# Moving V's stationary tiles by 352 bytes, dealing the second tokens' top-k between the gates of the first, and plain fp32 tiles of U beside top-k and the list only

## The chip, the cores and the metric

The kernel runs on one core of a Trainium2 chip. The metric is device time in microseconds (us) of the whole program, as the median of several executions. All engine names are those of the profile: PE is TensorE's matmul, PEld its weight loads, DVE is VectorE, ACT is ScalarE, POOL is GpSimd, SP is SyncE (here only a DMA queue).

## What is computed

Two transformer blocks on 256 tokens of width 2048, all in fp32. The change lies in one part of the first block, a mixture of 16,384 experts from which each token takes 128:

```python
q = (xn @ w_pq).reshape(B, S, 8, 2, 128)
s1, s2 = q[..., 0, :] @ sub_k1.T, q[..., 1, :] @ sub_k2.T      # 128 scores each, per head
v1, i1 = top_k(s1, 16);  v2, i2 = top_k(s2, 16)
cand = v1[..., :, None] + v2[..., None, :]                      # 256 per head
vs, ci = top_k(cand, 16)
eidx = i1[ci // 16] * 128 + i2[ci % 16];  gates = softmax(vs)
act = gelu(expert_u[eidx] . x)                                  # per token and chosen expert
y   = sum(act * gates * expert_v[eidx])
```

## The kernel before

**Three stages.** The program is a list of weight steps, each with a `prep` (load, split the fp32 weights into a high part `wh` on ACT and a low part `wl` on DVE) and an `mm` (the matmuls). A `Stream` issues `prep` of the next step and then `mm` of this one. Beside it runs a `Background`: after each step `strm.adv(n, bg, budget)` lets generators issue work until the costs that they `yield` use up the budget (a debt is carried over). So the order on every engine is fixed when the program is written, and each engine takes its instructions in that order. The stages that matter here:

- **U** (128 steps, one for each 128 experts): all experts' U rows against all 256 tokens. A step loads a tile of 1 MB by SP, transposes it on DVE (L804, `uT`, two buffers), and multiplies 16 blocks of 128 x 128 with the tokens. A *split* block takes three fp32r matmuls (L830 to L832: `wh` with `xh`, `wh` with `xl`, `wl` with `xh`). A *plain* block takes one fp32 matmul of `uT` with `xf` (L825), which the trace records as two passes. A plain step has 8 plain and 8 split blocks, so its `wh` and `wl` are one tile of 1024 columns; a split step has 16 split blocks and two such tiles. Steps 0 to 63 are plain (`NFU = 64`), 64 to 127 split. After the matmuls ACT and DVE make the first half of gelu from the accumulator (L835, L836), one step later the second half (L845, L846).
- **Beside U, in the background** (`peer_gen`): top-k of tokens 0 to 127 (`pairs_gen`, `topk_gen`; DVE only, save a few rows); then for each 64 tokens the gates (`gate_gen`: per 4 tokens one-hot tiles on DVE, L1045, and ACT, L1044, and their products on PE, L1053 and L1056) and the stores of them to DRAM (`store_gen`); top-k of tokens 128 to 255 stands beside the stores; then the list of chosen experts (`lists_gen`: a chain of small steps on DVE and PE, then 16 rounds of one-hots, L1136, and 8 products, L1170); then `p_gen`, one tile.
- **V** (109 steps and one more): rows of V for the listed experts are gathered by POOL, split, and used as the moving operand, 512 columns at a time, with the gated activations `ph` and `pl` (128 x 128) as stationary operand (L892 to L894: 1956 matmuls in this run). One step for both halves of the tokens has 24 matmuls, one for one half has 12.

Two budgets and costs set how much background work a step gets: 1.3 for the 8 first steps of U, 2.2 for the next 64, 2.0 for the other 56 until the list is done; a side of 128 scores costs 1.05, a head's 256 candidates 2.1, a block of gates 1.2.

**Places in SBUF.** Tiles lie one after another in a partition, in the order in which they are first asked for. Of the tiles that TensorE reads (bytes from the partition's start, as the built program lists them):

| tile | start | remainder by 64 |
|---|---|---|
| `wh`, `wl` (4 each) | 61216 + 4096 n, 77600 + 4096 n | 32 |
| `xh`, `xl` | 93984, 110368 | 32 |
| `ph`, `pl` (5 slots, tag `t1`) | 140736 + 1024 n | 0 |
| `pph`, `ppl` (tag `g2`, the projection of p) | 145856 + 2048 n | 0 |
| `xf`, `uT` | 202752; 210944 and 219136 | 0 |

The functions that the change touches, with the profile's line numbers:

Of the kernel before, what the change touches and what calls it, by code (L numbers as in the profile page):

```python
# [12 lines left out]
F32 = mybir.dt.float32  # L13
# [12 lines left out]
NE = 128  # L26
WB = 4
NF = 8
NFU = 64
WA, WB0, WB1 = 81, 28, 110  # L30


# [57 lines left out]
def tile_kernel(ctx: ExitStack, tc: tile.TileContext, A, out, dbg=None):  # L90
    nc = tc.nc
    V, S, T, G, SP = nc.vector, nc.scalar, nc.tensor, nc.gpsimd, nc.sync
# [18 lines left out]
    def bank(tag):  # L111
        return psp.tile([128, 512], F32, tag=tag, name=tag)
# [5 lines left out]
    def split(hi, lo, src):  # L118
        S.activation(hi, src, AF.Copy)  # L119
        V.tensor_tensor(lo, src, hi.bitcast(F32), op=OP.subtract)  # L120
# [81 lines left out]
    strm = Stream()  # L202
    bg = Background()

    class GStep:
        def __init__(self, g, k):
            self.g, self.k = g, k
            self.la = 3
            self.nw = 2 if g.ncols > 1024 else 1
# [93 lines left out]
    def flat(t):  # L303
        return t.rearrange("p a b -> p (a b)")
# [439 lines left out]
    tk = p2.enter_context(tc.tile_pool(name="tk", bufs=1))  # L744
# [8 lines left out]
    def t1(dt, name):  # L753
        return tk.tile([128, 256], dt, tag="t1", name=name, bufs=5)

    def g2(shape, dt=F32, name="g2"):
        return tk.tile(shape, dt, tag="g2", name=name, bufs=5)
# [16 lines left out]
    listI = tk.tile([128, 128], U32, name="listI")  # L774
    flag = tk.tile([1, 4], F32, name="flag")
    flagI = tk.tile([1, 1], I32, name="flagI")
    ubank = [bank("acc") for _ in range(3)]
    cnt = bank("acc")
    PP = {}
# [3 lines left out]
    class UStep:  # L783
        def __init__(self, f):
            self.f = f
            self.nf = NF if f < NFU else 0
            self.nw = 1 if self.nf == 8 else 2
            self.la = 1
            self.uT = None
            steps[f] = self  # L790

        def load(self):
            e = self.f * 128
            raw = raw_tile().rearrange("p (g c) -> p g c", g=4)
            src = A["expert_u"][0, e:e + 128, :].rearrange("(g j) (s q c) -> s q j g c", g=4, s=2, q=4)
            for i in range(8):
                s, q = i // 4, i % 4
                SP.dma_start(raw[32 * q:32 * q + 32, :, 256 * s:256 * s + 256], src[s, q])
            self.raw = raw
# [41 lines left out]
    def u_finish():  # L841
        if not pend:
            return
        f, x, a = pend.pop()
        S.activation(a, a, AF.Tanh, scale=GC3)  # L845
        V.scalar_tensor_tensor(a, a, 1.0, x, op0=OP.add, op1=OP.mult)  # L846
        G.dma_start(AG[f * 128:f * 128 + 128, 0:256], a)  # L847

    class VStep:
        la = 1  # L850
        nw = 2
# [79 lines left out]
    def p_gen():  # L931
        pin = g2([128, 2, 256], name="pin")
        S.dma_start(pin, A["p"][0, 0].rearrange("(b p) c -> p b c", p=128))
        PP["h"] = g2([128, 2, 256], F32R, "pph")
        PP["l"] = g2([128, 2, 256], F32R, "ppl")
        yield 3.0
        pt = bank("ms")
        for kk in range(2):
            for tb in range(2):
                T.transpose(pt[:, kk * 256 + tb * 128:kk * 256 + (tb + 1) * 128],  # L940
                            pin[:, tb, kk * 128:(kk + 1) * 128], ident)
        split(flat(PP["h"]), flat(PP["l"]), pt)
        yield
# [26 lines left out]
    def pairs_gen(tb, grp):  # L970
        for h2 in range(2):
            s = pq2[grp][:, tb, h2 * 512:h2 * 512 + 512].rearrange("p (a b) -> p a b", a=4)
            yield from topk_pair(tb, 4 * grp + 2 * h2, s)

    def top16(vals, idx, src, n):
        tmp = g2([128, 256], name="mr")[:, :n]
        V.max(vals[:, 0:8], src)
        V.max_index(idx[:, 0:8], vals[:, 0:8], src)
        V.match_replace(tmp, vals[:, 0:8], src, NEG)
        V.max(vals[:, 8:16], tmp)  # L980
        V.max_index(idx[:, 8:16], vals[:, 8:16], tmp)

    def topk_pair(tb, h0, s):
        vsel, i12, csel = vsel2[tb], i122[tb], csel2[tb]
        for i in range(2):
            hd = h0 + i
            v12 = tk.tile([128, 2, 16], F32, tag="v12", name="v12", bufs=2)
            ix = tk.tile([128, 2, 16], U32, tag="ix", name="ix", bufs=2)
            for side in range(2):
                top16(v12[:, side], ix[:, side], s[:, 2 * i + side, :], 128)  # L990
                V.tensor_copy(i12[side][:, hd, :], ix[:, side])
                yield 1.05
            cand = g2([128, 16, 16], name="cand")
            V.tensor_tensor(cand, v12[:, 0][:, :, None].to_broadcast([128, 16, 16]),
                            v12[:, 1][:, None, :].to_broadcast([128, 16, 16]), op=OP.add)
            top16(vsel[:, hd], csel[:, hd], cand.rearrange("p a b -> p (a b)"), 256)
            yield 2.1

    def topk_gen(tb):
        vsel, i12, csel = vsel2[tb], i122[tb], csel2[tb]  # L1000
# [37 lines left out]
    def gate_gen(t0, cost):  # L1038
        def one_hots(b):
            o1 = tk.tile([128, 4, 128], F32, tag="o1", name="o1", bufs=3)  # L1040
            o2 = tk.tile([128, 4, 128], F32, tag="o2", name="o2", bufs=3)
            for j in range(4):
                t = 4 * b + j
                S.activation(o2[:, j], iotaf, AF.Square, bias=eT[:, 1, t:t + 1])  # L1044
                V.tensor_scalar(o1[:, j], iotaf, eT[:, 0, t:t + 1], gT[:, t:t + 1], op0=OP.is_equal, op1=OP.mult)  # L1045
            S.activation(flat(o2), flat(o2), AF.Relu, scale=-1.0, bias=1.0)
            return o1, o2

        def products(b, oh):
            acc = bank("ms")  # L1050
            o1, o2 = oh
            for j in range(4):
                T.matmul(acc[:, j * 128:(j + 1) * 128], o2[:, j], o1[:, j], start=True, stop=True)  # L1053
            for j in range(4):
                t = (4 * b + j) % 128
                T.matmul(cnt[:, 128 * tb:128 * tb + 128], o2[:, j].bitcast(BF16)[:, 1::2], o1[:, j].bitcast(BF16)[:, 1::2],  # L1056
                         start=(t == 0), stop=(t == 127))
            return acc

        def place(b, acc):  # L1060
            S.activation(GB[:, :, 4 * b:4 * b + 4], acc.rearrange("p (t f) -> p f t", t=4), AF.Copy)

        tb, b0 = t0 // 128, t0 // 4
        ohs = []
        for i in range(2):
            ohs.append(one_hots(b0 + i))
            yield cost
        for b in range(16):
            acc = products(b0 + b, ohs.pop(0))
            if b < 14:  # L1070
                ohs.append(one_hots(b0 + b + 2))
            yield cost
            place(b, acc)

    def store_gen(t0, cost):
        dst = AG.rearrange("(f e) c -> e f c", e=128)
        for i in range(16):
            G.dma_start(dst[:, 8 * i:8 * i + 8, 256 + t0:320 + t0], GB[:, 8 * i:8 * i + 8, :])
            yield cost
# [104 lines left out]
    def both_gen(a, b, na, nb):  # L1184
        a, b = iter(a), iter(b)
        live = True
        while live:
            live = False
            for it, n in ((a, na), (b, nb)):
                for _ in range(n):  # L1190
                    c = next(it, None)
                    if c is not None:
                        live = True
                        yield c

    def chain(*gens):
        for g in gens:
            yield from g

    def peer_gen():  # L1200
        yield from chain(pairs_gen(0, 0), scores_gen(1), pairs_gen(0, 1), topk_gen(0))
        rest = chain(pairs_gen(1, 0), pairs_gen(1, 1), topk_gen(1))
        yield from gate_gen(0, 1.2)
        yield from both_gen(store_gen(0, 0.1), islice(rest, 14), 1, 1)
        yield from gate_gen(64, 1.2)
        yield from both_gen(store_gen(64, 0.1), rest, 1, 2)
        yield from gate_gen(128, 1.2)
        yield from store_gen(128, 0.6)
        yield from gate_gen(192, 1.2)
        yield from both_gen(store_gen(192, 0.2), lists_gen(), 1, 1)  # L1210
        yield from p_gen()

    def xs_gen():
# [28 lines left out]
    for k in range(8):  # L1242
        xs.one()
        strm.adv(1, bg, 0.7)
    bg.drain()
    bg.add(peer_gen())
    strm.adv(8, bg, 1.3)
    strm.adv(NFU, bg, 2.2)
    strm.adv(NE - NFU, bg, 2.0)
    u_finish()  # L1250
    bg.drain()

# [266 lines left out]
    for i in range(2):  # L1519
# [4 lines left out]
    rest = (tk.tile([128, 512], F32, tag="o1", name="ag", bufs=3),  # L1524
            big.tile([128, 2048], F32, tag="uT", name="rest", bufs=2), t1(F32R, "ph"), t1(F32R, "pl"))
# [116 lines left out]
```

## Time and profile before

| | |
|---|---|
| median of 3 runs | 2581.96 us (2581.3 to 2583.01) |
| the profiled execution | 2583.29 us, of which 2581.6 us is the span from first to last instruction |
| mean granted TensorE clock | 0.993 |
| PE busy | 2508.2 us, 97% |
| PEld busy | 2182.6 us, 85% |
| DVE busy | 1850.1 us, 72% |
| ACT busy | 1330.5 us, 52% |
| POOL busy | 398.4 us, 15% |

Matmuls are pipelined: the next one starts before the last one's recorded end, so PE counts as busy though it may start matmuls at different rates. Times within a stage are therefore read below as the distance from one start to the next. U's matmuls run from 391.9 to 1311.7 us, V's from 1326.0 to 1792.1 us.

### The profile page before, as it was taken

The numbers are of one execution on the slowest core, as the hardware profiler recorded it, in microseconds if no ns is written. First come the engines' busy times: TensorE is split into PE (matmuls) and PEld (weight loads), VectorE is DVE, ScalarE is ACT, GpSimd is POOL, SyncE is SP. The second block draws the span as 40 slices with busy tenths as digits, with TensorE's granted clock in tenths as the row PEclk, the third lists the DMA queues.
The fourth block names the chain that finished last, engine by engine and source line by source line (L and its number), as shares of the span: only waits on it lengthen the run. The fifth ranks groups of instructions, "written<-read, shape, count | busy, mean of one in ns | idle before, by whom it ended". The sixth has DMA issues, their size and how long they took to land. (4 is left out here: it accounts for less than half of the span.)

```text
span 2581.6 us, 37994 instructions
## 1 busy us (share of the span) xinstructions
PE 2508.2 (97%) x14001; PEld 2182.6 (85%) x14001; DVE 1850.1 (72%) x2851; ACT 1330.5 (52%) x2183; POOL 398.4 (15%) x529
## 2 busy tenths in 40 slices
PE   9999999999999999999899999999999999999999
PEld 8877778899898899898878888887888888888887
DVE  5665678987969989899957777776666456754564
ACT  6765543255362486645445555555555555544443
POOL 3000000001201202011035555552000000000000
PEclk9999999999999999999999999999999999999999
DMA  6644786665756768577679988997555545555664
GB/s 222 188 136 148 184 174 159 165 175 157 224 140 195 223 162 244 149 199 201 165 254 316 319 313 318 317 320 249 179 191 193 179 163 185 191 180 189 185 191 153
DMA packets 247154, 528.91 MB, mean 205 GB/s; under 512 B 27704, under 2 KB 163856, under 8 KB 232624
## 3 DMA queue, kind: packets, MB, share of 16 engines
q1 hardware_dynamic: 206864, 344.54, 45.3%
q0 software_dynamic: 36528, 179.96, 20.2%
q10 hardware_dynamic: 3568, 1.91, 0.3%
q8 instruction: 111, 1.82, 0.3%
q14 instruction: 83, 0.68, 0.1%
HBM read 488.55 MB, written 37.75 MB: 204 GB/s over the span
## 5 line engine op out<-in xcount | busy, mean ns | idle before, releaser
L120 DVE TENSOR_TENSOR wl<-raw,wh 128x1024 fp32r<-128x1024 f32 (+4 forms) x640 | 737.3, 1170 | 379.4 <-ACT wh L119 353.9
L119 ACT ACTIVATE wh<-raw 128x1024 fp32r<-128x1024 f32 (+4 forms) x640 | 637.2, 1010 | 380.5 <-PE acc L247 279.2
L832 PE MATMUL acc<-xh,wl 128*128 128x256 f32 x1536 | 438.8, 286 | 30.6 <-DVE wl L819 30.1
L245 PE MATMUL acc<-wh,xh 128*128 128x512 f32 (+2 forms) x1152 | 456.6, 396 | 6.0 <-ACT h L406 4.2
L830 PE MATMUL acc<-xh,wh 128*128 128x256 f32 x1536 | 451.3, 294 | 0.0
L246 PE MATMUL acc<-wl,xh 128*128 128x512 f32 (+2 forms) x1152 | 446.6, 388 | 0.7 <-DVE wl L120 0.7
L247 PE MATMUL acc<-wh,xl 128*128 128x512 f32 (+2 forms) x1152 | 447.1, 388 | 0.0
L831 PE MATMUL acc<-xl,wh 128*128 128x256 f32 x1536 | 435.5, 283 | 0.0
L804 DVE STREAM_TRANSPOSE uT<-raw 128x2048 f32<-128x2048 f32 x128 | 295.0, 2305 | 63.1 <-PE acc L825 53.8
L832 PEld LDWEIGHTS acc<-xh,wl 128*128 128x128 f32 x1536 | 295.2, 192 | 37.2 <-DVE wl L819 37.2
L830 PEld LDWEIGHTS acc<-xh,wh 128*128 128x128 f32 x1536 | 295.5, 192 | 1.9 <-issue 0.3
L831 PEld LDWEIGHTS acc<-xl,wh 128*128 128x128 f32 x1536 | 295.6, 192 | 1.7
L245 PEld LDWEIGHTS acc<-wh,xh 128*128 128x128 f32 x1152 | 217.4, 189 | 47.3 <-ACT h L406 4.6
L247 PEld LDWEIGHTS acc<-wh,xl 128*128 128x128 f32 x1152 | 217.2, 189 | 44.2
L246 PEld LDWEIGHTS acc<-wl,xh 128*128 128x128 f32 x1152 | 217.6, 189 | 41.9 <-DVE wl L120 1.7
L814 ACT ACTIVATE wh<-uT 128x1024 fp32r<-128x1024 f32 x192 | 195.5, 1051 | 87.9 <-DVE uT L804 87.8
L825 PE MATMUL acc<-xf,uT 128*128 128x256 f32 x1024 | 234.1, 382 | 3.9 <-ACT h L404 3.9
L819 DVE TENSOR_TENSOR wl<-uT,wh 128x1024 fp32r<-128x1024 f32 x192 | 224.5, 1195 | 8.2 <-ACT wh L814 8.1
L825 PEld LDWEIGHTS acc<-xf,uT 128*128 128x128 f32 x1024 | 190.8, 191 | 28.0 <-ACT h L404 4.3
L847 POOL DMA_DIRECT2D AG<-ga x128 | 70.0, 547 | 894.0 <-DVE ga L846 884.1
L835 ACT ACTIVATE ga<-acc 128x256 f32<-128x256 f32 x128 | 49.0, 383 | 306.7 <-PE acc L832 306.7
L868 POOL DMA_INDIRECT ag<-AG,listI x110 | 136.7, 1243 | 78.5 <-DVE pl L120 53.6
(446 smaller groups left out, 3737.2 us busy)
## 6 DMA issues: line engine op xcount, KB each, us to landing
raw<-in_expert_u_dram SPq DMA_DIRECT2D x1024, 128.0 KB, 3.6
raw<-in_w_in_dram SPq DMA_DIRECT2D x96, 1024.0 KB, 4.8
raw<-in_w_out_dram SPq DMA_DIRECT2D x32, 1024.0 KB, 5.7
raw<-in_w_pq_dram SPq DMA_DIRECT2D x64, 256.0 KB, 5.6
AG<-ga POOLq DMA_DIRECT2D x128, 128.0 KB
AG<-GB POOLq DMA_DIRECT2D x64, 256.0 KB
raw<-in_w_ple_gate_dram SPq DMA_DIRECT2D x16, 1024.0 KB, 5.6
raw<-in_w_in_dram SPq DMA_DIRECT2D x16, 544.0 KB, 3.8
```

Of the source, the lines that this page charges most:

```text
L119: S.activation(hi, src, AF.Copy)
L120: V.tensor_tensor(lo, src, hi.bitcast(F32), op=OP.subtract)
L245: T.matmul(o, xh, hi, start=first, stop=False)
L246: T.matmul(o, xh, lo, start=False, stop=False)
L247: T.matmul(o, xl, hi, start=False, stop=last)
L804: V.transpose(uT.rearrange("p b g j -> p g b j"), self.raw.rearrange("p g (b i) -> p g b i", i=32))
L814: S.activation(hi, self.uT[:, self.nf * 128 + i * n:self.nf * 128 + (i + 1) * n], AF.Copy)
L819: V.tensor_tensor(lo, self.uT[:, self.nf * 128 + i * n:self.nf * 128 + (i + 1) * n], hi.bitcast(F32), op=OP.subtract)
L825: T.matmul(acc, self.uT[:, k * 128:(k + 1) * 128], xf[:, k, :], start=(k == 0), stop=False)
L830: T.matmul(acc, hi[:, c], xt["h"][:, k, :], start=(k == 0), stop=False)
L831: T.matmul(acc, hi[:, c], xt["l"][:, k, :], start=False, stop=False)
L832: T.matmul(acc, lo[:, c], xt["h"][:, k, :], start=False, stop=(k == 15))
```

## The change

Three things are changed. A tile `pad` of 88 floats (352 bytes) is asked for ahead of the tiles of the tags `t1`, `g2` and `o1` and of `GB`, `xf` and `uT`, so that all of these lie 352 bytes later; `ph` and `pl` now start at 141088 + 1024 n, `pph` and `ppl` at 146208 + 2048 n, `xf` at 203104, `uT` at 211296 and 219488, each with a remainder of 32 by 64. `wh`, `wl`, `xh` and `xl` stay. POOL clears `pad` once.

Top-k of tokens 128 to 255 (`rest`) is no longer put beside the stores but dealt out, one piece after every two of the chain gates, stores, gates, stores of tokens 0 to 127. The budget is 2.0 throughout, and the costs are 1.3 for a side, 2.6 for candidates, 0.35 for a block of the first gates.

Whether a step of U is plain is now decided when it is prepared: it is, until the dealing is done; it is not beside the gates of tokens 128 to 255; it is again beside the last stores and the list, and not after the list.

```diff
-NFU = 64
...
+    pad = tk.tile([128, 88], F32, name="pad")
+    G.memset(pad, 0.0)
     ubank = [bank("acc") for _ in range(3)]
...
     class UStep:
         def __init__(self, f):
             self.f = f
-            self.nf = NF if f < NFU else 0
-            self.nw = 1 if self.nf == 8 else 2
+            self.plain = None
             self.la = 1
             self.uT = None
             steps[f] = self
+
+        @property
+        def nf(self):
+            if self.plain is None:
+                self.plain = NF if PP.get("plain", True) else 0
+            return self.plain
+
+        @property
+        def nw(self):
+            return 1 if self.nf == 8 else 2
...
                 V.tensor_copy(i12[side][:, hd, :], ix[:, side])
-                yield 1.05
+                yield 1.3
...
-            yield 2.1
+            yield 2.6
...
     def peer_gen():
         yield from chain(pairs_gen(0, 0), scores_gen(1), pairs_gen(0, 1), topk_gen(0))
         rest = chain(pairs_gen(1, 0), pairs_gen(1, 1), topk_gen(1))
-        yield from gate_gen(0, 1.2)
-        yield from both_gen(store_gen(0, 0.1), islice(rest, 14), 1, 1)
-        yield from gate_gen(64, 1.2)
-        yield from both_gen(store_gen(64, 0.1), rest, 1, 2)
+        first = chain(gate_gen(0, 0.35), store_gen(0, 0.1), gate_gen(64, 0.35), store_gen(64, 0.1))
+        yield from both_gen(first, rest, 2, 1)
+        PP["plain"] = False
         yield from gate_gen(128, 1.2)
         yield from store_gen(128, 0.6)
         yield from gate_gen(192, 1.2)
+        PP["plain"] = True
         yield from both_gen(store_gen(192, 0.2), lists_gen(), 1, 1)
+        PP["plain"] = False
         yield from p_gen()
...
     bg.add(peer_gen())
-    strm.adv(8, bg, 1.3)
-    strm.adv(NFU, bg, 2.2)
-    strm.adv(NE - NFU, bg, 2.0)
+    strm.adv(8 + NE, bg, 2.0)
```

Counted in the built program, 92 steps of U are plain and 36 split: 0 to 64 and 90 to 117 are plain, 65 to 89 and 118 to 127 split. Before, the list began at step 93 and ended at step 121; now it begins at step 89 or 90 and ends at 117. What a step holds is shown at two places, both on DVE.

**The first gates, DVE.** Before, a step beside the gates of tokens 0 to 63 holds the transpose (L804), one `wl` (L819), the two halves of gelu of two steps (L846, L836), and the one-hots of two blocks (L1045, four tokens in each):

```order
L804 STREAM_TRANSPOSE uT<-raw 128x4x16x32
L819 TENSOR_TENSOR wl<-uT,wh 128x1024
L846 SCALAR_TENSOR_TENSOR ga<-ga,acc 128x256
L836 SCALAR_TENSOR_TENSOR ga<-ga,acc 128x256
L1045 TENSOR_SCALAR o_5138<-iotaf,eT,gT 128x128 x4
L1045 TENSOR_SCALAR o_5159<-iotaf,eT,gT 128x128 x4
```

Now (the lines stand about ten later) a piece of top-k of tokens 128 to 255 follows the one-hots, here the first piece of a head, one side of 128 scores:

```order
L814 STREAM_TRANSPOSE uT<-raw 128x4x16x32
L829 TENSOR_TENSOR wl<-uT,wh 128x1024
L856 SCALAR_TENSOR_TENSOR ga<-ga,acc 128x256
L846 SCALAR_TENSOR_TENSOR ga<-ga,acc 128x256
L1055 TENSOR_SCALAR o_5492<-iotaf,eT,gT 128x128 x4
L1055 TENSOR_SCALAR o_5513<-iotaf,eT,gT 128x128 x4
L987 MAX v_5524<-h 128x8
L988 MAX_INDEX ix<-v_5524,h 128x8
L989 MATCH_REPLACE mr<-v_5524,h 128x128
L990 MAX v_5524<-mr 128x8
L991 MAX_INDEX ix<-v_5524,mr 128x8
L1001 CAST i_2673<-ix 128x16
```

Two blocks' one-hots and one piece of top-k now stand between two transposes; before, a step had the one or the other.

**The list, DVE.** Before, a step beside the list's rounds holds the transpose, two tiles of `wl`, two halves of gelu and the two one-hots of a round (L1136):

```order
L804 STREAM_TRANSPOSE uT<-raw 128x4x16x32
L819 TENSOR_TENSOR wl<-uT,wh 128x1024 x2
L846 SCALAR_TENSOR_TENSOR ga<-ga,acc 128x256
L836 SCALAR_TENSOR_TENSOR ga<-ga,acc 128x256
L1136 TENSOR_TENSOR o_11870<-iotaf,pq 128x1024
L1136 TENSOR_TENSOR o_11872<-iotaf,pq 128x1024
```

Now the step is plain:

```order
L814 STREAM_TRANSPOSE uT<-raw 128x4x16x32
L829 TENSOR_TENSOR wl<-uT,wh 128x1024
L856 SCALAR_TENSOR_TENSOR ga<-ga,acc 128x256
L846 SCALAR_TENSOR_TENSOR ga<-ga,acc 128x256
L1146 TENSOR_TENSOR o_11376<-iotaf,pq 128x1024
L1146 TENSOR_TENSOR o_11378<-iotaf,pq 128x1024
```

One `wl` of 1024 columns is gone from each such step of DVE; on PE, 24 split matmuls have become 8 plain ones.

## Rows read from the trace of the kernel before

**Rows 1.** Busy time by stretch (start:end, length, each engine, clock, DMA).

```profile
432.38:540.71 108.33, 102.92 (x643) 94.88 (x642) 101.52 (x194) 29.70 (x49) 8.13 (x15) 1.00 0.61 168
540.71:629.33 88.62, 88.62 (x638) 83.88 (x637) 62.70 (x110) 54.92 (x131) 5.95 (x11) 1.00 0.57 151
629.33:691.17 61.84, 57.92 (x363) 53.38 (x362) 58.92 (x153) 17.02 (x28) 16.57 (x22) 1.00 0.75 215
773.51:883.82 110.31, 103.22 (x670) 96.22 (x668) 107.03 (x191) 33.55 (x55) 17.73 (x26) 0.98 0.70 197
1070.86:1124.88 54.02, 46.24 (x364) 44.14 (x361) 43.10 (x68) 19.10 (x31) 6.93 (x11) 0.94 0.62 167
1124.88:1274.99 150.11, 138.34 (x1191) 135.19 (x1190) 146.95 (x144) 73.66 (x104) 22.73 (x34) 1.00 0.67 184
```

**Rows 2.** What PE waited for, 391 to 1312 us (total, times, longest).

```profile
PE acc L832 <- DVE wl L819: 30.1, 26, 2.6
...
PE ms L1146 <- DVE st L1148: 2.5, 1, 2.5
```

**Rows 3.** PE in order of time: a plain step, a block's products, a list round's.

```profile
540.71 3.61 PE L825 MATMUL acc<-xf,uT 128*128 128x256 f32 x16
...
544.27 0.28 PE L831 MATMUL acc<-xl,wh 128*128 128x256 f32 x1
...
547.02 0.38 PE L1028 MATMUL ms<-ident,e 128*128 128x128 f32 x2
...
553.67 1.05 PE L1053 MATMUL ms<-o,o 128*128 128x128 f32 x8
...
554.79 1.51 PE L825 MATMUL acc<-xf,uT 128*128 128x256 f32 x6
...
1232.52 0.62 PE L1170 MATMUL acc<-o,o 128*128 128x128 bf16 x8
1232.95 0.36 PE L830 MATMUL acc<-xh,wh 128*128 128x256 f32 x1
```

**Rows 4.** DVE in order of time: one side, one head's candidates, a plain step's share.

```profile
469.18 0.28 DVE L977 MAX8 v<-h 128x8 f32<-128x128 f32 x1
...
470.97 0.42 DVE L994 TENSOR_TENSOR cand<-v 128x256 f32<-128x256 f32 x1
...
473.67 2.30 DVE L804 STREAM_TRANSPOSE uT<-raw 128x2048 f32<-128x2048 f32 x1
...
477.66 0.28 DVE L977 MAX8 v<-h 128x8 f32<-128x128 f32 x1
```

**Rows 5.** DVE in order of time: one block's one-hots; one list step.

```profile
1062.71 1.12 DVE L1045 TENSOR_SCALAR o<-iotaf,eT,gT 128x128 f32<-128x128 f32 x4
1063.74 2.31 DVE L804 STREAM_TRANSPOSE uT<-raw 128x2048 f32<-128x2048 f32 x1
...
1230.85 2.30 DVE L804 STREAM_TRANSPOSE uT<-raw 128x2048 f32<-128x2048 f32 x1
1233.07 2.31 DVE L819 TENSOR_TENSOR wl<-uT,wh 128x1024 fp32r<-128x1024 f32 x2
...
1238.24 2.30 DVE L804 STREAM_TRANSPOSE uT<-raw 128x2048 f32<-128x2048 f32 x1
```

**Rows 6.** PE in order of time: matmuls of 512 columns with `pph` and with `xh`.

```profile
1322.36 0.39 PE L245 MATMUL ms<-wh,pph 128*128 128x512 f32 x1
...
1323.06 0.39 PE L245 MATMUL ms<-wh,pph 128*128 128x512 f32 x1
...
1999.88 0.39 PE L245 MATMUL acc<-wh,xh 128*128 128x512 f32 x1
...
2006.00 0.39 PE L245 MATMUL acc<-wh,xh 128*128 128x512 f32 x1
```

**Rows 7.** Busy time by stretch: the head of V, V at length.

```profile
1312.00:1330.00 18.00, 12.11 (x34) 8.83 (x35) 6.91 (x10) 8.19 (x14) 8.35 (x10) 0.77 0.59 222
1330.00:1760.00 430.00, 430.00 (x1841) 345.89 (x1840) 307.34 (x415) 238.51 (x311) 227.09 (x207) 1.00 0.90 317
```

## The prediction, made before the changed kernel ran

> **What bounds the kernel now.** I read the busy times by stretch first, to find where PE, which is busy nearly throughout, is short of work; then what it waited for; then the order of time on PE and DVE, to price a step.
>
> A plain step of U takes 6.31 us on PE when nothing is late (540.71 to 547.02), a split matmul 0.1196 us (23 of them from 544.27 to 547.02), so a split step 48 x 0.1196 = 5.74 us: a plain step costs 0.57 us more. One block's products take 1.12 us, a list round's eight 0.43 us [rows 3]. Against these prices four stretches of U are too long [rows 1]:
> - first top-k, 16 plain steps: 108.33 - 16 x 6.31 = 7.4 us lost;
> - second top-k beside the first stores, 9 plain steps: 61.84 - 56.8 = 5.1 us;
> - second top-k beside the second stores, 13 plain and 3 split steps: 110.31 - 82.0 - 17.2 - 0.4 for other matmuls = 10.7 us;
> - the list's rounds, 22 split steps: 150.11 - 126.3 - 15 x 0.43 - 1 for other matmuls = 16.4 us.
>
> In these DVE is busy 94 to 98% of the time, and the wait that PE shows is L832 for `wl` from DVE (L819), 26 times, 30.1 us [rows 2]. Less is recorded as wait than is lost, because a matmul's record outlasts its turn. Beside gates alone (540.71 to 629.33) PE has no idle time and DVE is busy 71%. So DVE is the bound beside top-k and the list, and has time to spare beside the gates. The list's first steps (1070.86 to 1124.88) lose 7.8 us of idle time and, at a granted clock of 0.94, some 3.2 us more: 11.0 us. There PE stands behind its own small matmuls, which wait for DVE one at a time (L1146: 2.5 us [rows 2]).
>
> V loses nothing to waits: 430.00 of 430 us busy, 1841 matmuls, so 0.2336 us each [rows 7]. The matmuls of the same shape with `xh` as stationary tile follow each other at 6.12 / 27 = 0.2267 us [rows 6].
>
> **The first top-k.** On DVE a side takes 1.80 us (469.18 to 470.97), a head's candidates 2.70, so a head 6.30; the rest of a plain step takes 3.99 (473.67 to 477.66) [rows 4]. Before, a head costs 4.2 of a budget of 2.2, so 1.91 steps: DVE 1.91 x 3.99 + 6.30 = 13.9 us, PE 12.0, 0.98 us too much in each step. Now it costs 5.2 of 2.0, 2.6 steps: 16.7 against 16.4, 0.10 too much, 2.1 us for 8 heads. DVE may owe PE something before PE waits, since `wl` is made one step ahead: in the 9 steps above it fell 8.8 us behind and PE lost 5.1, so about 3.5 us are free. So 2.1 us stay unseen but for bursts; I leave 1 us of the 7.4 (0 to 4).
>
> **Dealing out the second top-k.** One head is three pieces, with six blocks of gates between: cost 5.2 + 6 x 0.35 = 7.3, that is 3.65 steps. DVE: 3.65 x 3.99 + 6.30 + 6 x 1.03 (one-hots of a block, 1062.71 to 1063.74 [rows 5]) = 27.0 us. PE: 3.65 x 6.31 + 6 x 1.12 = 29.8. PE is the longer by 2.7 us a head, so the pieces lie behind its matmuls. Beside the stores a head costs 5.2 + 6 x 0.1 = 5.8, 2.9 steps: DVE 17.9, PE 18.3. Of the 15.8 us I leave 1.5, for bursts (0 to 15; the upper end is a rival below). What queues behind a piece on DVE is the next transpose and `wl`, for which PE waits a step later, and the one-hots of blocks that come two later.
>
> **Plain steps beside the list.** A list step takes 7.39 us now, 1230.85 to 1238.24, all of it DVE [rows 5]. A plain step drops one `wl` of 1024 columns (two record 2.31): 7.39 - 1.15 = 6.24 us on DVE, against 6.31 + 0.43 = 6.74 on PE. The 16.4 us go (0 to 3 stay). Of the 11.0 us of the list's first steps most are a chain: the small matmuls still wait for DVE, which comes to them 1.15 us sooner while a step lasts 0.57 longer. I leave 8 (5 to 11).
>
> **What the plain steps cost.** 92 instead of 64: 28 x 0.57 = 16.0 us more for PE.
>
> U in sum: 7.4 + 15.8 + 11.0 + 16.4 = 50.6 us lost before, 1 + 1.5 + 8 + 0 = 10.5 after; 40.1 saved less 16.0 gives **-24 us** (-2 if 4, 15, 11 and 3 stay; -30 if only 5 stay in all).
>
> **Moving `ph` and `pl`.** No operation changes, only the place. Two groups of matmuls with the same moving tiles `wh` and `wl` differ: `pph` from 1322.36 to 1323.06 takes 0.70 / 3 = 0.2333 us each, as V's `ph` does at 0.2336, `xh` 0.2267 [rows 6, 7]. Data traffic is no reason: DMA is at 0.59 about `pph`, at 0.90 in V. What `ph`, `pl`, `pph` and `ppl` share is a start with remainder 0 by 64, where `xh`, `xl` have 32, as they all have after the change. Bounds: 0, if something else sets the pace, and 1956 x 0.0069 = 13.5 us. I take the row of `xh`, to which they become alike: **-13 us**. Gathers keep pace: a DMA share of 0.90 would become 0.93.
>
> The Trainium skill speaks against this: "TensorE: Matmul & The Clock Gate", section "Back-to-back issue gap", gives the distance of matmuls at full clock as columns / 2.4 plus 2.5 ns, 215.7 ns for 512 columns, with no term for the stationary tile's place. By it the move is worth nothing and the sum is -24 us. The trace has 226.7 and 233.3 ns, neither of them that figure, and a difference that the rule has no room for, so I go by the rows.
>
> **At no cost.** Clearing `pad` is one small POOL instruction ahead of U; POOL is busy 8 of 108 us beside top-k [rows 1], and exposed it would cost under 1 us. `xf` and `uT` move too; a plain block's two passes keep their price, or else each of 92 plain steps pays 16 times what a pass gains or loses. The same tiles, stores and gathers are moved.
>
> Sum: -24 - 13 = -37 against the profiled 2583.29 us: 2546. The median of the runs lies 1.3 us below that execution, so **2545 us**.
>
> **Rivals.**
> - *The place does nothing, or the gathers hold V at its old pace* (14%). For it: 6.6 ns is little, and V is the stretch with most DMA. Against it: `pph`. Time: 2582 - 24 = 2558. The rule of the Trainium skill cited above would be this rival.
> - *U gains half* (15%). The dealt pieces come in bursts: a step can hold two blocks' one-hots and a side and candidates, 3.99 + 2.06 + 4.50 = 10.6 us of DVE against 8.55 of PE, and if each such burst stops PE, some 12 us of the 15.8 stay. For it: before, such pairs of pieces each stopped PE. Against it: there DVE was already behind. Time: 2545 + 12 = 2557.
> - *Both* (5%): 2570.
> - *The products wait* (3%, the slower side). PE takes its matmuls in order, and L1053 needs one-hots that DVE may have queued behind a piece of top-k. If each of the 32 first blocks waits for one piece of 2.70 us, U loses 86 us, and the time is 2631. It decides from (37 + 5) / 32 = 1.3 us a block on. Against it: one-hots are issued two blocks ahead, so a whole step of U lies between them and their products, and in the rows before no product waits.
> - *U's extra PE work eats all* (3%): no change. It needs 24 of the 40 us to stay.
>
> **How the numbers follow.** The forecast has 60%, 2536 to 2552 by its own terms: the low end with 5 us left in U and 13.5 in V, the high end with 4 more us in top-k and 3 in the rounds. The range for 8 in 10 takes in the first two rivals: 2535 to 2563. 0.2% (5 us) is about what a measurement of this kernel tells from no change. Faster 0.94 (60 + 14 + 15 + 5), same 0.03, slower 0.03.
>
> **What would show it.** Right: V's matmuls at 0.2267 us from start to start; beside the list steps of 6.3 to 6.8 us and no wait of PE for `wl`; beside the dealt top-k PE idle for under 3 us; 92 plain steps at 6.31. Wrong: V still at 0.233; L1053 (now ten lines later) among PE's waits; waits for `wl` among the first gates; a list round of 7 us or more, bound by something that is not `wl`.

## The result, and the profile after

The changed kernel takes 2553.07 us (median of 4 runs, 2550.0 to 2555.31), the kernel before 2582.41 (2581.3 to 2583.01): a ratio of 0.9887, with a 95% interval of 0.9875 to 0.9899. That is 29 us, where 37 were forecast. The profiled execution took 2553.34 us with a span of 2551.6, 30.0 less than before, at the same mean granted clock of 0.993.

PE in order of time shows where they are: U's first and last matmul, two of V six apart, and V's last (columns as in [rows 3], with the idle time ahead and what ended it).

```profile
395.47 0.79 PE L835 MATMUL acc<-xf,uT 128*128 128x256 f32 x1 [7.30 <-ACT h L403]
...
1292.48 0.28 PE L842 MATMUL acc<-xh,wl 128*128 128x256 f32 x1
...
1499.74 0.39 PE L903 MATMUL ms<-wl,ph 128*128 128x512 f32 x1
...
1501.10 0.39 PE L903 MATMUL ms<-wl,ph 128*128 128x512 f32 x1
...
1762.54 0.39 PE L904 MATMUL ms<-wh,pl 128*128 128x512 f32 x1
```

U begins 3.6 us later than before (391.9), lasts 897.0 instead of 919.8 us (-22.8), V's first matmul stands at 1306.54, and V lasts 456.0 instead of 466.1 (-10.1). The rest, 0.7 us, lies outside these stretches; together that is the 30.0.

The busy times by stretch answer to [rows 1] and [rows 7] (start:end, length, PE, PEld, DVE, ACT, POOL with their counts, granted clock, DMA share, GB/s): 16 plain steps of the first top-k, the dealt top-k, the list's first steps (89 to 97), its rounds (98 to 117), step 118, and 400 us of V.

```profile
447.76:549.99 102.23, 101.39 (x642) 94.53 (x641) 99.47 (x174) 29.50 (x48) 8.69 (x16) 1.00 0.69 184
562.96:840.66 277.70, 277.70 (x1906) 261.57 (x1905) 251.35 (x529) 137.15 (x310) 47.50 (x68) 1.00 0.69 190
1027.92:1095.50 67.58, 61.35 (x415) 56.99 (x414) 44.89 (x73) 16.77 (x30) 9.42 (x14) 0.97 0.62 169
1095.50:1230.11 134.61, 134.61 (x930) 125.65 (x929) 116.09 (x114) 52.32 (x77) 20.82 (x31) 1.00 0.65 186
1230.11:1240.69 10.58, 7.87 (x55) 7.67 (x53) 9.47 (x9) 2.97 (x5) 0.54 (x1) 0.84 0.96 224
1330.00:1730.00 400.00, 399.31 (x1759) 329.51 (x1758) 295.02 (x396) 224.89 (x297) 199.06 (x198) 1.00 0.91 324
```

PE has no idle time in 278 us of dealt top-k and none in the list's rounds, though DVE is busy 91% in the one and 86% in the other. Step 118 took 10.58 us where a split step takes 5.8. V has 1759 matmuls in 400 us, 0.2274 us each, against 0.2336 [rows 7]. What PE waited for from 391 to 1312 us (total, times, longest) answers to [rows 2]:

```profile
PE acc L835 <- ACT h L403: 7.3, 1, 7.3
PE acc L842 <- DVE wl L829: 3.6, 2, 2.7
...
PE ms L1156 <- DVE st L1158: 2.9, 1, 2.9
...
PE ms L1129 <- DVE tz L1127: 1.4, 1, 1.4
PE ms L1107 <- DVE cls L1101: 1.4, 1, 1.4
```

The 26 waits for `wl` have become 2. The longest is now ahead of U: 7.3 us, where the wait at the same place was 3.9 before:

```profile
PE acc L825 <- ACT h L404: 3.9, 1, 3.9
```

### The profile page after: what moved, and what is told of

It reads as the page before. It is cut to its first block, busy times and chain, and to the rows that moved or that the text cites. A ratio compares the mean times of both kernels' runs of the same rounds, so it can differ in the third digit from the quotient of the medians.

```text
span 2551.6 us, 37437 instructions
## 1 busy us (share of the span) xinstructions
PE 2500.6 (98%) x13776; PEld 2182.4 (86%) x13777; DVE 1824.6 (72%) x2823; ACT 1297.0 (51%) x2155; POOL 379.1 (15%) x530
## 3 DMA queue, kind: packets, MB, share of 16 engines
q0 software_dynamic: 36528, 179.96, 20.5%
## 5 line engine op out<-in xcount | busy, mean ns | idle before, releaser
L840 PE MATMUL acc<-xh,wh 128*128 128x256 f32 x1312 | 390.6, 298 | 0.0
L842 PE MATMUL acc<-xh,wl 128*128 128x256 f32 x1312 | 371.5, 283 | 3.6 <-DVE wl L829 3.6
L841 PE MATMUL acc<-xl,wh 128*128 128x256 f32 x1312 | 371.5, 283 | 0.0
L835 PE MATMUL acc<-xf,uT 128*128 128x256 f32 x1472 | 337.3, 382 | 7.3 <-ACT h L403 7.3
L835 PEld LDWEIGHTS acc<-xf,uT 128*128 128x128 f32 x1472 | 274.5, 191 | 41.9 <-ACT h L403 7.7
L842 PEld LDWEIGHTS acc<-xh,wl 128*128 128x128 f32 x1312 | 251.6, 192 | 4.0 <-DVE wl L829 4.0
L841 PEld LDWEIGHTS acc<-xl,wh 128*128 128x128 f32 x1312 | 251.9, 192 | 2.4
L840 PEld LDWEIGHTS acc<-xh,wh 128*128 128x128 f32 x1312 | 251.5, 192 | 2.5
L829 DVE TENSOR_TENSOR wl<-uT,wh 128x1024 fp32r<-128x1024 f32 x164 | 192.8, 1193 | 8.1 <-ACT wh L824 8.0
L118 ACT ACTIVATE ph<-ag 128x128 fp32r<-128x128 f32 (+1 forms) x110 | 39.9, 362 | 195.8 <-DVE ag L881 195.8
```

The costliest lines, as they stand in the source:

```text
L829: V.tensor_tensor(lo, self.uT[:, self.nf * 128 + i * n:self.nf * 128 + (i + 1) * n], hi.bitcast(F32), op=OP.subtract)
L835: T.matmul(acc, self.uT[:, k * 128:(k + 1) * 128], xf[:, k, :], start=(k == 0), stop=False)
L840: T.matmul(acc, hi[:, c], xt["h"][:, k, :], start=(k == 0), stop=False)
L841: T.matmul(acc, hi[:, c], xt["l"][:, k, :], start=False, stop=False)
L842: T.matmul(acc, lo[:, c], xt["h"][:, k, :], start=False, stop=(k == 15))
```

## The experiments

### V's place

Does the place alone do it, and what about the place?

```diff
 e1_pad_only (from the kernel before)
+    pad = tk.tile([128, 88], F32, name="pad")
+    G.memset(pad, 0.0)
 e2_pad_320 (from the changed kernel)
-    pad = tk.tile([128, 88], F32, name="pad")
+    pad = tk.tile([128, 80], F32, name="pad")
 e6_all_32 (from the kernel before, ahead of every other tile)
+    shift = const.tile([128, 8], F32, name="shift")
+    G.memset(shift, 0.0)
```

> The kernel before plus only the pad of 352 bytes (it lies ahead of ph, pl, pph, ppl, xf, uT, which then start with remainder 32 by 64). Theory 'place': V's matmuls go from 0.2333 to 0.2267 us each, 1956 x 0.0066 = -12.7 us, less the 2.6 us of new waits and slower-clock starts that V shows in the changed kernel, so about -10 to -13 us: 2569 to 2572; U as before, 920 us. Rival 'place does nothing' (V got faster because something else in the schedule changed): 0, V's distance stays 0.2333, time 2582.

> The changed kernel with a pad of 320 instead of 352 bytes, so the same tiles move by nearly as much but start with remainder 0 by 64, as before the change. Theory 'remainder': V back at 0.2333 us each, +10 to +13 us against the changed kernel, 2563 to 2566. Rival 'any other place will do' (a clash with a certain other tile): V stays at 0.2267, time 2553.

> The kernel before with 32 bytes put ahead of all tiles: every tile moves by 32, so wh, wl, xh, xl go from remainder 32 to 0, and ph, pl, pph, ppl, xf, uT from 0 to 32. Theory 'the stationary tile's start has to be 32': V (stationary ph at 32) falls to 0.2267 (-13 us), the GEMMs (stationary xh at 0) rise from 0.2267 to 0.2333 (some 4,300 matmuls of 512 columns, +28 us), U's split matmuls stay or rise by up to 6.6 ns each (0 to +30): 2597 to 2627. Rival 'moving and stationary have to have the same remainder': GEMMs stay at 0.2267 (both 0), V stays at 0.2333 (0 and 32 instead of 32 and 0): 2582. Rival 'the moving tile's start has to be 32': V and GEMMs all slower.

V in the same 400 us, first of the kernel before with the pad alone:

```profile
1330.00:1730.00 400.00, 400.00 (x1761) 330.46 (x1761) 295.21 (x397) 225.77 (x298) 206.86 (x199) 1.00 0.92 326
```

then of the changed kernel with a pad of 320 bytes:

```profile
1330.00:1730.00 400.00, 400.00 (x1716) 321.32 (x1715) 285.52 (x386) 222.22 (x290) 210.73 (x193) 1.00 0.91 317
```

and of the kernel before with all tiles moved by 32:

```profile
1330.00:1730.00 400.00, 400.00 (x1716) 321.75 (x1715) 284.90 (x387) 222.62 (x290) 211.15 (x193) 1.00 0.91 318
```

The pad alone gave 2571.31 us, a ratio of 0.9957 (0.9940 to 0.9973), and V at 0.2271 us a matmul, while U took 919.8 us as before: the place does it, and the gathers keep pace with it, at a DMA share of 0.92. With 320 bytes V is back at 0.2331 and the time at 2565.69 (0.9936, 0.9920 to 0.9953), 12.6 us above the changed kernel. So not just any other place will do.

The third run overturned my reason. With `ph` at remainder 32 and all of `wh`, `wl`, `xh`, `xl` at 0, V did not get faster (1716 matmuls), and the GEMMs did not get slower. PE in order of time in a GEMM of this run:

```profile
1996.48 0.39 PE L248 MATMUL acc<-wh,xh 128*128 128x512 f32 x1
...
2002.60 0.39 PE L248 MATMUL acc<-wh,xh 128*128 128x512 f32 x1
```

27 matmuls in 6.12 us, 0.2267 as in [rows 6]. The time was 2581.50 (0.9999, 0.9989 to 1.0008). So it is not the place of `ph` alone; what fits all three runs is how the two operands stand to each other. Two more pads tell by which unit:

```diff
 e7_pad_32 (from the changed kernel)
-    pad = tk.tile([128, 88], F32, name="pad")
+    pad = tk.tile([128, 8], F32, name="pad")
 e11_pad_96 (from the changed kernel)
-    pad = tk.tile([128, 88], F32, name="pad")
+    pad = tk.tile([128, 24], F32, name="pad")
```

> The changed kernel with a pad of 32 bytes: ph starts at 140768 + 1024 n and wh at 61216 + 4096 n. The two have the same remainder by 64 (32), but not by 128 (96 and 32), 256 or 512; with 352 bytes they agree by 512 as well. Theory 'the remainders by 64 have to agree': V's matmuls 0.2267 us apart, time 2553. Rival 'they have to agree by 128 or more': 0.2333, time 2565.

> The changed kernel with a pad of 96 bytes: ph starts 256 bytes from wh's start by 512. So far V's matmuls stood 0.2267 us apart where the distance of the two starts is 0 by 512, 0.2290 where it is 192, 0.2333 where it is 160 or -32. Theory 'the distance counts by 256 or less': 0.2267. Rival 'by 512': 0.2290, as at 192. Rival 'it is not the distance': 0.2333.

With 32 bytes (2558.08 us, one run):

```profile
1330.00:1730.00 400.00, 400.00 (x1749) 327.90 (x1748) 292.51 (x394) 225.40 (x295) 212.06 (x197) 1.00 0.91 322
```

With 96 bytes (2554.38 us, one run):

```profile
1330.00:1730.00 400.00, 399.99 (x1762) 330.09 (x1761) 295.70 (x397) 224.91 (x297) 197.74 (x198) 1.00 0.91 325
```

In the first of these neither of the two expected levels came: 0.2287 lies between them. All kernels together, by how far `ph` starts behind `wh`, taken by 512:

| kernel | start of `ph` less start of `wh`, by 512 | matmuls in 400 us | us each |
|---|---|---|---|
| before | 160 | 1712 | 0.2336 |
| all moved by 32 | 160 | 1716 | 0.2331 |
| pad 320 | 480 | 1716 | 0.2331 |
| pad 32 | 192 | 1749 | 0.2287 |
| pad 96 | 256 | 1762 | 0.2270 |
| changed, pad alone | 0 | 1759, 1761 | 0.2274, 0.2271 |

Within a level the figures differ only by a few matmuls at the lower clock at the window's start and by a few waits. Taken from start to start, without gaps of 0.25 us and more, the mean distance in V is 0.2333 us at 160 and 480 (before, all moved by 32, pad 320), 0.2289 at 192, and 0.2267 to 0.2268 at 0 and 256.

Distances of 0 and 256 are alike and best, 192 loses a third of the gain, 160 and 480 all of it. A distance of 128 was not tried, so whether it counts by 128 or by 256 is open, and why it counts at all is not shown. A pad moves `ph` against all tiles that stayed, not against `wh` alone; that `wh` is the one that counts is argued from `xh`, which lies at distance 0 from `wh` and kept 0.2267 us in both places.

### The dealing and the plain list

```diff
 e5_list_split (from the changed kernel)
         yield from gate_gen(192, 1.2)
-        PP["plain"] = True
         yield from both_gen(store_gen(192, 0.2), lists_gen(), 1, 1)
 e8_plain_only (from the kernel before; nf and nw are read when a step is prepared)
+                self.plain = NF if self.f < NFU or PP.get("plain") else 0
...
+        PP["plain"] = True
         yield from both_gen(store_gen(192, 0.2), lists_gen(), 1, 1)
+        PP["plain"] = False
 e12_costs_only (from the kernel before)
-                yield 1.05
+                yield 1.3
...
-            yield 2.1
+            yield 2.6
...
-    strm.adv(NFU, bg, 2.2)
-    strm.adv(NE - NFU, bg, 2.0)
+    strm.adv(NE, bg, 2.0)
```

> The changed kernel with split steps beside the list (28 plain steps fewer). By the terms of the prediction: 28 x 0.57 = 16.0 us less of PE's extra work, but the 16.4 us that the rounds lost and about 3 us of the list's first steps come back: +3 us, 2556. Rival 'the plain list is where most of U's gain is' (the dealing would then have gained little): +10 us or more, 2563. Rival 'the plain list costs more than it gives': 2548 or less.

> The kernel before with one part of the change alone: plain steps beside the list (27 more plain steps; order, costs, budgets and places as before). By the terms of the prediction: 16.4 of the rounds and 3 of the first steps saved, 27 x 0.57 = 15.4 us of extra work on PE: -4 us, 2578. Rival 'most of U's gain is here': -15 us, 2567. Rival 'the extra work eats it': 2582 or more.

> The kernel before with the new costs and budgets alone: 1.3 for a side, 2.6 for candidates, budget 1.3 for the eight steps ahead of U and 2.0 after; order, gates' costs, plain rule (64 first steps) and places as before. Top-k then fills more steps, and by the built program's order 8 of the list's 16 rounds come after U's last matmul. Theory 'the costs stop the stalls, the dealing makes room for it': the 22 us of stalls ahead of the list go, but some 25 us of list stand alone behind U: 2575 to 2585, and the dealing is what turns it into a gain. Rival 'the costs are the gain': 2562 or less.

With a split list the time was 2550.78 us (0.9883, 0.9866 to 0.9899), not told apart from the changed kernel. Plain steps beside the list alone, in the kernel before, gave 2584.22 (1.0009, 0.9999 to 1.0019). In neither direction do they gain; the -4 that I had expected is excluded by the second interval. The busy times of the split list show why: first steps, rounds, step 118, at the same steps as in the stretches above.

```profile
1029.15:1093.66 64.51, 59.17 (x471) 57.24 (x469) 54.52 (x81) 24.27 (x38) 9.45 (x14) 0.95 0.67 179
1093.66:1232.44 138.78, 126.68 (x1091) 123.31 (x1089) 137.11 (x133) 69.17 (x96) 20.80 (x31) 1.00 0.68 182
1232.44:1240.17 7.73, 6.36 (x54) 6.15 (x53) 7.08 (x8) 2.96 (x5) 0.54 (x1) 1.00 1.11 233
```

Against these the plain list takes 4.2 us less in the rounds (134.61 for 138.78), 3.1 more in the first steps (67.58 for 64.51) and 2.9 more in step 118: +1.8 in all.

Beside the list the trace has 27 plain steps, 91 to 117, not the 28 that the text ahead of the prediction (90 to 117) and the first expectation count; 65 stand ahead of it, one more than before.

The costs alone left the time where it was, 2582.93 (1.0004, 0.9995 to 1.0013), as the theory had it, but one half of its mechanism failed. What PE waited for in this run, from 388 to 1330 us:

```profile
PE acc L832 <- DVE wl L819: 30.5, 24, 3.6
PE acc L1170 <- ACT o L1174: 9.9, 6, 2.8
```

The waits for `wl` did not go (30.1 in [rows 2]); they moved. Here are 16 plain steps of the first top-k (8 to 23) and five split steps (76 to 80) in this run:

```profile
446.36:548.52 102.16, 101.38 (x642) 94.52 (x641) 98.75 (x194) 29.50 (x48) 8.67 (x16) 1.00 0.67 182
931.42:967.79 36.37, 30.06 (x242) 29.05 (x241) 35.50 (x45) 13.86 (x21) 5.44 (x8) 1.00 0.68 185
```

The plain steps take 102.16 us, as in the changed kernel, so beside them the new costs did stop the stalls. But top-k, dearer by its costs, now reaches into the split steps, and in these it stops PE again (steps 78 to 80 last 7.17 us for 5.76 us of matmuls). And PE waits for the list's one-hots behind U (L1170), since half of the list stands there: V begins 29 us behind U's last matmul instead of 14. So the costs need the dealing: it puts DVE's pieces where PE has gates to multiply, ends top-k while U's steps are still plain, and leaves steps for the list. By difference, 2550.78 - 2571.31, the dealing with its costs and budgets is worth -20.5 us. Two kernels between these were not run, the dealing with the old costs, and the new costs with plain steps to the end of top-k; how the 20.5 us divide between order and costs is thus not shown.

### Ahead of U, and the load of p

Two losses of the changed kernel were not in the forecast.

```diff
 e3_budget (from the changed kernel)
-    strm.adv(8 + NE, bg, 2.0)
+    strm.adv(8, bg, 1.3)
+    strm.adv(NE, bg, 2.0)
 e4_p_pool (from the changed kernel)
-        S.dma_start(pin, A["p"][0, 0].rearrange("(b p) c -> p b c", p=128))
+        G.dma_start(pin, A["p"][0, 0].rearrange("(b p) c -> p b c", p=128))
```

> The changed kernel with the budget of before, 1.3 instead of 2.0, in the eight steps that stand ahead of U (the last eight of the w_pq GEMM, which the document up to the prediction counted as U's). Theory 'the larger budget delays U': in these steps DVE then has about one side of top-k (1.80 us) beside 1.1 us for wl on 2.72 us of PE, and U's first matmul comes at 391.9 again instead of 395.5; the pieces that are left over fall into U's plain steps, which have 0.1 us per step too much already, so part comes back: -1 to -3.6 us, 2549 to 2552. Rival 'the work is only moved': U's first top-k takes 3.6 us longer and the time stays at 2553.

> The changed kernel with one edit: the load of p (pin, ahead of p_gen) is issued by POOL instead of ACT. In the changed kernel step 118, the first split step after the list, loses 4.37 us; ahead of it DVE stands idle for 4.52 us for the raw tile, and SP's queue, which had not issued a load since 1213, had waited 13.1 us for the load of pin, which ACT issued at 1223.48. Theory 'the two queues share their completion counts, so SP waits for ACT's load': SP issues on, DVE's idle time goes, step 118 at 5.8 to 6.5 us, -3 to -4.4 us: 2549 to 2550. Rival 'the change from plain to split itself costs it, since twice as much wl is wanted': step 118 stays at 10 us, time 2553.

**Ahead of U.** The first transposes of U on DVE, in order of time, in the kernel before:

```profile
387.85 4.51 DVE L804 STREAM_TRANSPOSE uT<-raw 128x2048 f32<-128x2048 f32 x2 [0.20 <-DMA raw<-in_expert_u_dram]
```

in the changed kernel:

```profile
391.46 4.49 DVE L814 STREAM_TRANSPOSE uT<-raw 128x2048 f32<-128x2048 f32 x2
```

what ACT does behind the first of them:

```profile
393.87 1.06 ACT L824 ACTIVATE wh<-uT 128x1024 fp32r<-128x1024 f32 x1 [16.36 <-DVE uT L814]
394.83 2.04 ACT L403 ACTIVATE h<-acc 128x512 f32<-128x512 f32 x4
```

and with the budget of 1.3, beside U's first matmul on PE:

```profile
384.70 4.49 DVE L814 STREAM_TRANSPOSE uT<-raw 128x2048 f32<-128x2048 f32 x2
...
388.71 1.56 PE L835 MATMUL acc<-xf,uT 128*128 128x256 f32 x6 [1.78 <-ACT h L403]
```

The transposes stand behind the pieces of top-k, U's first `wh` on ACT stands behind the first transpose, and behind that `wh` stand the last four results of the GEMM ahead of U (L403). By the profile it is these that U's first matmul waits for; it starts 4.0 us behind the start of the transposes in all three traces (387.85 before, 391.46, 384.70). With fewer pieces ahead, U began 6.8 us sooner than in the changed kernel, and sooner than the 391.9 that I had expected, but took 4.3 us longer, so 2.5 us were left at U's end. The time was 2548.6 us (0.9870, 0.9854 to 0.9887), 4.5 less than the changed kernel, with intervals that overlap. Of the 4.9 us between the two profiled spans 2.8 lie in V, which took 453.2 us in this execution and which the edit does not touch; there 13 of V's matmuls stood 0.427 us apart, in the changed kernel 22.

**Step 118.** In the changed kernel, what SP's queue waited for from 1200 to 1245 us:

```profile
SPq L808 <- DMA pin<-in_p_dram: 13.1, 1, 13.1
```

and in order of time ACT's load of `pin`, the transpose on DVE and the matmul on PE that follow:

```profile
1223.48 0.37 ACTq L943 DMA_DIRECT2D pin<-in_p_dram  x1
...
1229.75 2.31 DVE L814 STREAM_TRANSPOSE uT<-raw 128x2048 f32<-128x2048 f32 x1 [4.52 <-DMA raw<-in_expert_u_dram]
...
1233.22 0.39 PE L842 MATMUL acc<-xh,wl 128*128 128x256 f32 x1 [2.71 <-DVE wl L829]
```

PE was idle for 2.7 us, and then, from 1234.5 to 1238.0 us, at a granted clock of 0.51, its matmuls stood some 0.21 us apart instead of 0.12, which makes up the rest of the loss.

U's loads need nothing of p. But in the built program each load of SP and ACT waits for one of eight completion counts (semaphores) that they take in turn, and the one that follows `pin` on its count is a load of U, written two steps ahead. It waited until `pin`, which ACT reached only at 1223.48, had landed 2.8 us later. The Trainium skill says what goes wrong without such a wait ("DMA: Bandwidth & Descriptors", section "Why a DMA increments its semaphore by 16 and not by 1"): a count is fed by many engines, so with two transfers in flight on one count it can reach its value before the first has landed, and each in flight should have its own. No run here shows what would happen without the wait; the trace shows what it costs. With `pin` on POOL, whose loads take other counts in these traces, the wait is gone from SP's list; what SP waited for there from 1200 to 1250 us is only

```profile
SPq L808 <- DVE uT L814: 18.0, 8, 3.1
```

and step 118 is one of 6.78 us:

```profile
1231.42:1238.20 6.78, 6.37 (x54) 6.17 (x53) 6.78 (x7) 2.85 (x5) 0.57 (x1) 1.00 0.75 195
```

The step gained 3.8 us, as expected; the time was 2550.54 us (0.9884, 0.9868 to 0.9901), whose interval does not tell it from the changed kernel by itself. The same wait stood in the kernel before (12.6 us for SP), where it cost step 122 2.3 us, and stands in the one with a split list (14.0 us for SP), whose step 118 took 7.73: behind plain steps the same wait cost more. Why is not shown.

### The list's first steps, and the sum

```diff
 e9_rounds: the edits of e3_budget and e4_p_pool, and
         yield from gate_gen(192, 1.2)
-        PP["plain"] = True
         yield from both_gen(store_gen(192, 0.2), lists_gen(), 1, 1)
...
+        PP["plain"] = True
         for f0 in range(0, NE, 8):
 e10_spread: e9_rounds, and in lists_gen (one hand-over of six)
         V.tensor_scalar(cls[:, 3], cls[:, 3], -1.0, 1.0, op0=OP.mult, op1=OP.add)
+        yield 2.0
         pt = bank("ms")
         for c in range(4):
             T.matmul(pt[:, c:c + 1], cls[:, c], wt[:, 512:513], start=True, stop=True)
```

> The changed kernel with three edits: budget 1.3 in the last eight steps of the w_pq GEMM (the single edit gave 2548.6), p loaded by POOL (the single edit gave 2550.5), and plain steps beside the list's rounds only, not beside its first steps and the stores ahead of it. There the changed kernel takes 67.6 us for steps 89 to 97 and the one with a split list 64.5, so the plain steps cost 3.1 us and save nothing. Theory 'the three add up': 2553.1 - 4.5 - 2.5 - 3.1 = 2543. Rival 'the plain first steps are needed, since DVE comes late into the rounds': the first rounds wait for wl again, 2546 or more.

> The kernel of e9_rounds with one more edit: in the list's first steps every hand-over between DVE and a small matmul lies across the end of a step, so that PE finds its operands made in the step before (the sum of the costs stays 14). Theory 'the first steps lose by a chain within a step': PE stands behind DVE and DVE behind PE there, and the 9 us that steps 89 to 94 lose fall to 2 or 3: -6 to -7 us against e9_rounds, 2536 to 2537. Rival 'they are short of DVE': no more than -1.

The three edits gave 2540.48 us (0.9838, 0.9825 to 0.9852), 2.5 less than their terms together; the spread list gave 2532.51 (0.9810, 0.9797 to 0.9823), 8.0 less again where 6 to 7 were expected, and 20.6 us below the changed kernel. The list's first steps (here 92 to 100), with the chain within a step:

```profile
1040.06:1103.88 63.82, 56.69 (x458) 55.11 (x457) 53.83 (x81) 23.25 (x37) 9.79 (x14) 0.97 0.68 179
```

and spread over the steps, where ten steps (92 to 101) and the first round fit into the same time:

```profile
1039.14:1102.75 63.61, 61.13 (x515) 60.00 (x513) 58.70 (x86) 26.33 (x42) 12.12 (x17) 1.00 0.79 207
```

PE's idle time fell from 7.1 to 2.5 us though DVE did more in it, and the granted clock from 0.97 back to 1.00. So these steps were held by a chain, not by DVE's work. DVE's part of the background stands behind gelu's first half, which waits for the step's matmuls (L846 for `acc`), and PE's small matmuls stand right behind the same matmuls; a hand-over inside one step of this program is therefore late.

## Why the prediction was right, and where it was not

The time, 2553.07 us, lies within the 2535 to 2563 of the prediction, but 1 us outside the 2536 to 2552 that it gave the forecast by its own terms (added up again, their low end is 2539). The direction and the two main mechanisms, less work on DVE where it was the bound and a shorter distance in V, came as forecast. That the sum came out as near as it did is in part luck, as the terms show:

- **First top-k: 7.4 us lost before, 1 left.** 16 plain steps now take 102.23 us, 1.3 above 16 x 6.31. This was right.
- **Second top-k: 15.8 lost, 1.5 left.** None is left: PE idles 0 of 277.70 us. The balance by head (27.0 us of DVE against 29.8 of PE, a share of 0.91) was right, since DVE is busy 251.35 of the 277.70 us, and the bursts of the rival "U gains half" did not come. L1063 is not among PE's waits, so the products did not wait either. Over the steps up to the list, U lost 27.3 us before and 4.4 after (each step's length in the trace less 6.32 us for a plain step, 5.76 for a split one and 1.17 for each 12 small matmuls, a block of gates). These -22.9 us are about the whole gain of U.
- **List's rounds: 16.4 lost, 0 left, for 22 x 0.57 of plain work.** This was right: -3.9 by these terms, -4.2 against the split list.
- **List's first steps: 11.0 lost, 8 left.** Some 9 stayed in the steps 89 to 94, and the plain steps cost 3.1 us there for nothing. I had named the chain but not asked where in a step its links stand; e10_spread shows that this was most of it.
- **Not in the sum: step 118.** It lost 4.4 us. Of the same wait 2.3 us were there before, in step 122, behind the list's rounds, where the prediction did not look.
- **Not in the sum: the steps ahead of U.** The step that failed is my reading of the first call of `strm.adv` behind `bg.add(peer_gen())`: I took its 8 steps for U's first. They are the last of the GEMM by `w_pq`, 2.72 us each, and the budget of 2.0 there puts more top-k ahead of U's first transpose: 3.6 us.
- **U in sum:** -24 forecast, -22.8 from U's first to last matmul. The list's share of it, -3.4, came out as +1.8 against a split list, and the dealing's as more than forecast, so the sum is nearer than its terms; that is luck.
- **V: -13.** The distance is 0.2267 us (six matmuls from 1499.74 to 1501.10) instead of 0.2333, and over 1956 matmuls that is -12.9 us. Of this 2.8 came back. 22 matmuls instead of 16 were 0.427 us apart, at V's start and in its last step, and there are two short waits for `wl` and some smaller ones; with a pad of 320, where V is slow again, no two matmuls between V's start and its last step are over 0.3 us apart, so the slower matmuls had hidden these waits. The size was thus right and the term mis-sized by what a faster PE runs into. The cause I gave, the remainder of the stationary tile, is wrong: it held for the row of `xh` only because `xh` and `wh` stand alike. So the forecast of V is in part luck too: 352 bytes bring the distance from `wh` to 0 by 512, while another pad that also gives a remainder of 32 (32 bytes) has only two thirds of the gain.
- **The rule cited against it**, of the Trainium skill ("TensorE: Matmul & The Clock Gate", section "Back-to-back issue gap"), has no term for place and gives some 216 ns, for a matmul by itself. The measurements disagree: one kernel has 0.2333, 0.2289 or 0.2267 us by its pad, and no run came to that figure.

What came back in V stands in two views of the changed kernel: V's start by busy times, with a granted clock of 0.76,

```profile
1306.00:1320.00 14.00, 12.99 (x44) 10.12 (x45) 8.76 (x13) 9.32 (x15) 6.40 (x7) 0.76 0.91 344
```

and what PE waited for from 1314 to 1745 us:

```profile
PE acc L903 <- DVE wl L119: 0.7, 2, 0.5
```

Of the sum of 37, 24 + 13, the runs thus found 22.8 + 10.1, less 3.6 lost ahead of U, which makes 29.3; 0.7 us more lie outside U and V.

## What to carry to other kernels

Background work on a busy engine belongs beside steps whose matmuls outlast it, and its cost must count what each step really has to spare; a change of costs alone only moved the stall to another place. Put a hand-over between two engines across the end of a step, not inside it. Ask of every load that stands in a round of completion counts with others what is issued behind it, and compare the starts of the two operands of a long run of matmuls.

## What the runs showed of the hardware that I had not expected

- Matmuls of 512 columns (fp32r) follow each other after 0.2267 us where the operands' starts differ by 0 or 256 bytes (by 512), 0.2289 at 192 and 0.2333 at 160 and 480. In these runs it is the distance and not the place: moving both by 32 bytes changed nothing.
- A load on ACT's queue held SP's loads up for 13.1 us, through a completion count that the two share; the same load issued by POOL, on another count, did not.
